# A state recurrence in three levels, meta keys' exponentials in PSUM, and pads between the experts' tiles

## The chip, the core and the metric

One core of a Trainium2 chip runs the whole kernel. The metric is device time in microseconds (us) from the first to the last instruction of one execution, as a median of runs.

## The reference, cut to what matters

```python
h = layer_norm(concat([16 meta tokens, x]))                 # (2064, 1024)
q, k, v, u, g_attn, g_ssm = split(h @ w_in)
y_attn = softmax(q k^T / 8) v                               # 8 heads, 2064 keys, the last 16 are the meta tokens
for direction in range(2):                                  # S5 layer: 32 groups x 64 complex states
    abar, bbar = zoh_discretise(a, log_dt, b)
    s_t = abar * s_{t-1} + bbar u_t                         # the state recurrence, forward and backward
    y += Re(c s)
y_ssm = gelu(y) * sigmoid(gelu(y) @ w_glu + b_glu)
h = layer_norm(alpha h + (sig(g_attn)(y_attn w1) + sig(g_ssm)(y_ssm w2)) @ w_o)
out = layer_norm(alpha h + expert_choice_moe(h))            # 16 experts, each takes its best 256 tokens
```

## The kernel before

The program is written out by hand: each engine executes its instructions in the order in which the Python code issues them, and waits only for data and for buffers.

- **Phase A** (`phase_a`) normalises 17 tiles of 128 tokens, projects them to q, k, v and u. `u_mm` (L267) makes u with matmuls of 128x128 weights against 256 columns. A float32 product is three matmuls: high part by high part, low by high, high by low.
- **Gates** (`gates`) are 64 steps of 24 matmuls of 512 columns (L1169) with nothing else to wait for than their weights' split: ACT casts the high part (L1126), DVE subtracts the low part (L1127). The generator gives control back after every 4 matmuls; such a piece is called a quantum here, and there are 384 of them. `drive` puts as many quanta behind each step of another phase as the step's `yield` says (1 if it says nothing), so the gates are TensorE's filling work in the phases `ssm` and `glu`, and in the first part of `phase_b`; what is left is issued before the main part of `phase_b`.
- **`ssm`** loads and discretises the parameters (SP's queue, L712 to L726, and DVE); makes for each chunk of 16 tokens its contribution to the state (`v_item`: 64 items, evacuated by ACT at L918 into `VA`, 129 chunks x 2 directions x 32 groups; the real half stands on partitions 0 to 63, the imaginary one on 64 to 127); runs the recurrence over the chunks (`scan`, 127 steps of 5 DVE instructions of 64 elements, one quantum behind each); and makes the outputs (`y_item`, L1009 and L1013, with the kernels of `k_item`, whose first five are combined on POOL, L879 to L881, while the scan runs). After the scan stands `yield 10`.
- **`phase_b`** sweeps 32 units (4 query blocks x 8 heads) in 9 steps each: 8 steps with 256 keys and a ninth (i = 8) with the 16 meta keys. A step makes the scores in a PSUM tile `pS` (two buffers), ACT takes the exponential into `pe` (L490) and a float16 copy `ph` (L502; in step 3 DVE makes it, L500), and `pl` = `pe` - `ph` is made by POOL (L508) for 256 keys and by DVE (L511) for the meta keys, two steps later. `max_mm` (L449) and `max_red` (L455) find the next unit's row maxima; `pend` holds at most two of them. `PROG` writes the order of a step out: S and T are the scores, M a `max_mm`, P a quarter of the products with v, and / lets DVE take the pending maxima and then one entry of its queue `vq`.
- **`experts`** takes 16 experts in turn. Weights are loaded in pieces of 1 MB, split by ACT (`wh`, L1629) and DVE (`wl`, L1630). Gate and up products (L1721) have 256 columns of `xh`/`xl` as the moving operand and 128x128 of `wh`/`wl` as weights; down products (L1749) have 256 columns of `wh`/`wl` moving and 128x128 of `hh`/`hl` as weights. All tiles in the pools `e_w` and `e_x` are whole multiples of 4 KiB per partition, and these pools follow each other directly, so any two of them start a whole number of 4 KiB apart.

Of the kernel before, what the change touches and what calls it, by code (L numbers as in the profile page):

```python
# [10 lines left out]
F32 = mybir.dt.float32  # L11
F32R = mybir.dt.float32r
# [28 lines left out]
def row_bcast(ap, n, parts=128):  # L41
    return bass.AP(tensor=ap.tensor, offset=ap.offset, ap=[[0, parts], [1, n]])
# [7 lines left out]
def kernel(ctx, tc, x, meta, ln_in_g, ln_in_b, w_in, q_norm_g, k_norm_g,  # L50
# [321 lines left out]
    def phase_b(c):  # L372
# [100 lines left out]
        def scores(n, i, a):  # L473
            g = units[n][1] // 4
            w = 2 if i < NT // 2 else 1
            m = 128 if i < NT // 2 else NM
            if a >= w:
                return
            if a == 0:
                PS[n, i] = ps.tile([128, 2, 512], F32, name="pS")  # L480
            p = PS[n, i]
            k0 = 128 * (2 * i + a)
            PE.matmul(p[:m, a], K2[g][:, k0:k0 + m], Q[n][1], start=True, stop=False)  # L483
            PE.matmul(p[:m, a], K1[g][:, k0:k0 + m], Q[n][0], start=False, stop=True)  # L484
            if a < w - 1:
                return
            e = pp.tile([128, 2, 512], F32, name="pe", bufs=PR["PE"])
            hi = pp.tile([128, 2, 512], F16, name="ph", bufs=PR["PH"])
            lo = pp.tile([128, 2, 512], F16, name="pl", bufs=PR["PH"])
            A.activation(e[:m, :w], p[:m, :w], AF.Exp, bias=ebias[:m], scale=HD ** -0.5)  # L490
            P[n, i] = e, hi, lo, m, w

        PR = dict(HI=(3,), LOV=(16,), LAG=4, LEAD=3.75, PE=7, PH=5, LOS=2,
                  PROG=("SMTM/PPP/P/M/", "SMTMPP/PP/MM/M", "SMTM//PPPP/M/M"))
# [8 lines left out]

        def split_lo(n, i, on_v):
            e, hi, lo, m, w = P[n, i]
            hs = [a for a in range(w) if (2 * i + a in PR["LOV"]) == on_v]
            if len(hs) == 2 and not on_v:
                PL.tensor_tensor(lo[:m, :w], e[:m, :w], hi[:m, :w], op=OP.subtract)  # L508
                return []
            eng = V if on_v else PL  # L510
            return [lambda a=a: eng.tensor_tensor(lo[:m, a], e[:m, a], hi[:m, a], op=OP.subtract) for a in hs]  # L511

# [79 lines left out]
        for s in range(len(steps) + LAG):  # L592
            want = min(NC, int((s + LEAD) * 20 // NP))
            live = s < len(steps)
            if live:
                n, i = steps[s]
                if i == 0 and n + 2 < NU:
                    load_q(n + 2)
            if 0 <= s - PR["LOS"] < len(steps):
                for g in split_lo(*steps[s - PR["LOS"]], False):  # L600
                    g()
                vq += split_lo(*steps[s - PR["LOS"]], True)
            if 0 < s <= len(steps) and steps[s - 1][1] in PR["HI"]:
# [31 lines left out]
            if live:  # L635
                split_hi(n, i, False)
            if s == len(steps) - 1:
                c2.close()
# [30 lines left out]
    def ssm(c):  # L669
# [6 lines left out]

        VA = tb.tile([128, 2, 32, CB + 2], F32, name="VA")
        PL.memset(VA[:, 1, :, CB:CB + 1], 0.0)
        bbar = tb.tile([128, 2, 32, 16], F32, name="bbar")
        lo_t = tb.tile([128, 2, 2, 32, T + 1], F32, name="lo_t")  # L680
        cst = tb.tile([128, 2, DG, 16], F32, name="cst")
        lt = tb.tile([128, 2, 2, 32], F32, name="lt")
        st = tb.tile([128, 2, 2, 32], F32, name="st")
        dd = tb.tile([16, 32], F32, name="dd")
# [16 lines left out]
        with pool(name="s_i", bufs=1) as ti:  # L701
# [8 lines left out]
            for i, src in enumerate((ssm_a_re, ssm_a_im)):  # L710
                for j in range(2):
                    SP.dma_start(raw[:, i, j], src.rearrange("l d g p -> (l d g) p"))  # L712
            ldt = new()
            SP.dma_start(ldt, row_bcast(ssm_log_dt, DG))
            SP.dma_start(dd, ssm_d.rearrange("l g h -> h (l g)"))
            craw = new((128, 8, 2, 2, 64), tag="gco")
            for x in range(2):
                for y in range(2):
                    src = (ssm_c_re, ssm_c_im)[x ^ y]
                    SP.dma_start(craw[:, :, x, y], src.rearrange("l d g h p -> (l d g h) p")  # L720
                                 .rearrange("(n p) q -> p n q", p=128))
# [142 lines left out]
            do(V.tensor_copy, lt, Lr[:, :, T])  # L864
            do(V.tensor_scalar, lt[64:, 1], lt[64:, 1], -1.0, None, op0=OP.mult)
            for ri in range(2):
# [5 lines left out]
            yield from flush(4)  # L872
        up = c1.enter_context(pool(name="s_u", bufs=2))
        bstv = bst.rearrange("p r (d g) h -> p r d g h", d=2)
        cstv = cst.rearrange("p r (d g) h -> p r d g h", d=2)
# [18 lines left out]
        def make_ws(i):  # L894
# [5 lines left out]
            WS[i] = ws  # L900

        def v_item(k, d, g):
            if g == 3 and d == 0 and k < 7:
                load_u(k + 1, True)
            if g == 0 and 2 * k + d < 15:
                make_ws(2 * k + d + 1)
            pw = pp.tile([128, KT, 128], F32, name="pA")
            for kt in range(KT):
                PE.transpose(pw[:, kt], WS[2 * k + d][:, g, 8 * kt:8 * kt + 8].rearrange("p j h -> p (j h)"), idf)
            yield  # L910
            wi = s1.tile([128, KT, 128], F32, name="wi", bufs=3)
            A.copy(wi, pw)
            yield
            pv = pp.tile([128, 512], F32, name="pB", bufs=3)
            for kt in range(KT):
                PE.matmul(pv[:, :CB], wi[:, kt], U[k][:, kt, g], start=(kt == 0), stop=(kt == KT - 1))
            yield
            A.copy(VA[:, d, 4 * k + g, :CB], pv[:, :CB])  # L918

        load_u(0, True)  # L920
        make_ws(0)
        yield
        for i, _ in enumerate(pipe(v_item(k, d, g) for k in range(8) for d in range(2) for g in range(4))):
            yield (i + 1) % 2
        c1.close()
        c1 = ExitStack()
        kp = c1.enter_context(pool(name="s_k", bufs=1))
        up = c1.enter_context(pool(name="s_v", bufs=2))
        CL, MM = {}, {}

# [29 lines left out]
        def load_mm(k):  # L960
            mm = kp.tile([128, KT, 2, TH], F32, name="mm", bufs=3)
            for g in range(2):
                for kt in range(KT):
                    src = kf_d[2 * k + g]
                    SP.dma_start(mm[:, kt, g], bass.AP(tensor=src.tensor, offset=src.offset + 8 * kt * 16,
                                                       ap=[[16, 8], [NL * 16, 16], [1, TH]]))
            MM[k] = mm

        def slot(f, bk, p0, p1):
            a = VA[p0:p1, :, :, f]  # L970
            ap = [list(z) for z in a.ap]
            ap[1][0] += bk - f
            return bass.AP(tensor=a.tensor, offset=a.offset, ap=ap)

        def scan():
            for m in range(1, CB - 1):
                f0, f1 = m - 1, m
                b0, b1 = CB - m, CB - 1 - m
                tt(st[:, 0], lt[:, 0], slot(f0, b0, 0, 128), OP.mult)
                tt(st[:64, 1], lt[64:, 1], slot(f0, b0, 64, 128), OP.mult)  # L980
                tt(st[64:, 1], lt[:64, 1], slot(f0, b0, 0, 64), OP.mult)
                cur = slot(f1, b1, 0, 128)
                tt(cur, cur, st[:, 0], OP.add)
                tt(cur, cur, st[:, 1], OP.add)
                yield

        kk = pipe((k_item(k, False) for k in range(5)), every=22)
        for _ in scan():
            next(kk, None)
            yield  # L990
        for _ in kk:
# [6 lines left out]
        def y_item(k):  # L998
            if k % 2 == 0 and k < 14:
                load_u(k // 2 + 1, False)  # L1000
            py = pp.tile([128, 2, KT, CX], F32, name="pB", bufs=3)
            mm, cl = MM.pop(k), CL.pop(k)
            u = U[k // 2]
            for g in range(2):
                ug = 2 * (k % 2) + g
                for mt in range(KT):
# [3 lines left out]
                    for d in range(2):  # L1010
                        w = cl[:, d, g, 1 - d:T + 1 - d].rearrange("p j h -> p (j h)")
                        a0 = 2 * d
                        PE.matmul(py[:, g, mt], w[:, cs_], VA[:, d, 2 * k + g, a0:a0 + CX], start=False, stop=d == 1)  # L1013
                yield
            t = kp.tile([128, 2, KT, CX], F32, name="yt", bufs=3)
            A.activation(t, py, AF.Square)
            yield
            V.tensor_scalar(t, t, 0.044715, 1.0, op0=OP.mult, op1=OP.add)
# [590 lines left out]

    def experts(c, pos, inf):  # L1610
        wp = c.enter_context(pool(name="e_w", bufs=3))
        E0 = E - 7
# [35 lines left out]
        yield first_split()  # L1648
        xp = c.enter_context(pool(name="e_x", bufs=2))
        sm = c.enter_context(pool(name="e_m", bufs=2))  # L1650
        pp = c.enter_context(pool(name="e_p", bufs=2, space=PSUM))
# [50 lines left out]
        def trans_out(e, i, p):  # L1702
            if i == 0:
                XT[e] = (xp.tile([128, 8, CAP], F32R, name="xh"), xp.tile([128, 8, CAP], F32R, name="xl"))
            hi, lo = XT[e]
# [351 lines left out]
```

## Time and profile before

| | us |
|---|---|
| median of 3 runs | 3305.42 |
| lowest, highest run | 3301.82, 3309.93 |
| the profiled execution | 3306.01 |
| its span (first to last instruction) | 3303.9 |

The span is what the trace covers; the profiled execution is 2.1 us longer than its span and 0.6 us longer than the median. Engines in the rows: PE is TensorE's matmuls, PEld its weight loads, DVE VectorE, ACT ScalarE, POOL GpSimd, SP SyncE, and a q behind a name the engine's queue of issues and waits. L12 is line 12 of the kernel before.

### The profile page before, as it was taken

The page shows a single profiled execution, that of the slowest core. Times are in us where ns is not written, and L with a number is a line of the kernel's source. Part 1 is how long each engine was busy: PE and PEld are TensorE (multiplying, and loading weights), DVE is VectorE, ACT ScalarE, POOL GpSimd, SP SyncE. Part 2 cuts the span into 40 slices and gives each one's busy share as a digit, 9 for nine tenths or more (in the row PEclk, how much of TensorE's full clock was granted, in tenths as well). Part 3 has the DMA queues.
Part 4 walks back from the last instruction along what each step waited for, and adds up shares of the span by engine and source line. Part 5 has one row for each costly group of instructions (what it writes and reads, how often), then busy time and mean ns, then how long its engine had stood idle before and what let it go on. Part 6 is the DMA issues. An engine that isn't in the chain of part 4 may idle for free. (4 is left out here: it accounts for less than half of the span.)

```text
span 3303.9 us, 56603 instructions
## 1 busy us (share of the span) xinstructions
PE 3045.8 (92%) x22805; PEld 2686.9 (81%) x22805; DVE 2287.5 (69%) x4206; ACT 1557.3 (47%) x2197; POOL 1000.7 (30%) x633
## 2 busy tenths in 40 slices
PE   6999996788999999999999997599999999999997
PEld 5887785566777777777778886599999999999997
DVE  7884779985357777777556665666566665778875
ACT  2222341112349889898732222344444444556552
POOL 3221050033039989898820001000011001112221
PEclk9999998899999999999999998799999999999998
DMA  6666521544730101012086652366666666878773
GB/s 223 192 193 213 132 77 53 163 131 139 217 109 21 33 21 33 17 36 86 27 254 191 175 169 104 110 210 203 204 205 214 208 204 217 262 235 281 262 255 133
DMA packets 464502, 513.03 MB, mean 155 GB/s; under 512 B 47568, under 2 KB 387728, under 8 KB 463856
## 3 DMA queue, kind: packets, MB, share of 16 engines
q1 hardware_dynamic: 435104, 422.31, 40.4%
q0 software_dynamic: 19232, 69.53, 7.2%
q10 hardware_dynamic: 9904, 17.57, 1.5%
q8 instruction: 179, 2.93, 0.4%
q14 instruction: 83, 0.68, 0.1%
HBM read 385.59 MB, written 123.76 MB: 154 GB/s over the span
## 5 line engine op out<-in xcount | busy, mean ns | idle before, releaser
L1721 PE MATMUL pg<-xh,wh 128*128 128x256 f32 x2048 | 586.3, 286 | 15.7 <-DVE sg L1729 9.7
L1721 PE MATMUL pg<-xh,wl 128*128 128x256 f32 x2048 | 582.8, 285 | 0.5 <-DVE wl L1630 0.5
L1721 PE MATMUL pg<-xl,wh 128*128 128x256 f32 x2048 | 582.9, 285 | 0.0
L1630 DVE TENSOR_TENSOR wl<-wr,wh 128x2048 fp32r<-128x2048 f32 x189 | 433.1, 2292 | 215.1 <-ACT wh L1629 215.1
L508 POOL TENSOR_TENSOR pl<-pe,ph 128x1024 f16<-128x1024 f32 x256 | 554.6, 2201 | 79.7 <-DVE ph L500 67.1
L455 DVE TENSOR_REDUCE mx<-pm 128x1 f32<-128x412 f32 (+1 forms) x640 | 365.5, 584 | 153.6 <-PE pm L449 138.3
L1721 PEld LDWEIGHTS pg<-xh,wh 128*128 128x128 f32 x2048 | 396.6, 194 | 17.0 <-issue 12.2
L1721 PEld LDWEIGHTS pg<-xh,wl 128*128 128x128 f32 x2048 | 396.6, 194 | 0.7 <-DVE wl L1630 0.7
L1721 PEld LDWEIGHTS pg<-xl,wh 128*128 128x128 f32 x2048 | 396.8, 194 | 0.0
L1629 ACT CAST wh<-wr 128x2048 fp32r<-128x2048 f32 x189 | 358.4, 1896 | 7.3 <-DMA wr<-in_w_up_e_dram 5.7
L1169 PE MATMUL pg<-gh,gwh 128*128 128x512 f32 x1024 | 344.8, 412 | 12.9 <-ACT gg L1140 6.9
L490 ACT ACTIVATE pe<-pS,ebias 128x1024 f32<-128x1024 f32 (+1 forms) x288 | 306.6, 1065 | 63.3 <-PE pS L484 62.6
L1749 PE MATMUL pd<-wh,hh 128*128 128x256 f32 x1024 | 292.6, 286 | 5.2 <-ACT ye L1767 2.7
L1749 PE MATMUL pd<-wh,hl 128*128 128x256 f32 x1024 | 290.5, 284 | 0.7 <-DVE hl L1736 0.7
L1749 PE MATMUL pd<-wl,hh 128*128 128x256 f32 x1024 | 290.2, 283 | 0.0
L1169 PE MATMUL pg<-gh,gwl 128*128 128x512 f32 x512 | 213.0, 416 | 63.0 <-DVE gwl L1127 62.9
L449 PE MATMUL pm<-k,q 128*128 128x412 f32 (+1 forms) x640 | 237.7, 381 | 33.4 <-DVE mx L455 29.0
L502 ACT CAST ph<-pe 128x1024 f16<-128x1024 f32 (+1 forms) x256 | 254.2, 993 | 18.3
L1169 PEld LDWEIGHTS pg<-gh,gwh 128*128 128x128 f32 x1024 | 200.1, 198 | 59.8 <-ACT gg L1140 8.8
L525 PEld LDWEIGHTS <-ph 128*128 128x128 f16 (+1 forms) x2176 | 190.5, 97 | 65.0 <-issue 61.8
L525 PE MATMUL po<-v,ph 128*128 128x129 f16 (+1 forms) x2176 | 234.0, 222 | 0.7 <-ACT t L533 0.7
L483 PE MATMUL pS<-q,k 128*128 128x512 f32 (+1 forms) x544 | 232.7, 428 | 0.0
(412 smaller groups left out, 6848.7 us busy)
## 6 DMA issues: line engine op xcount, KB each, us to landing
wr<-in_w_gate_e_dram SPq DMA_DIRECT2D x64, 1024.0 KB
wr<-in_w_up_e_dram SPq DMA_DIRECT2D x64, 1024.0 KB
wr<-in_w_down_e_dram SPq DMA_DIRECT2D x64, 1024.0 KB
gwr<-in_w_in_dram SPq DMA_DIRECT2D x32, 512.0 KB
gh<-ht_d SPq DMA_DIRECT2D x64, 256.0 KB
gt_d<-gg ACTq DMA_DIRECT2D x64, 256.0 KB
gt<-gt_d SPq DMA_DIRECT2D x32, 512.0 KB
q<-q_d SPq DMA_DIRECT2D x96, 128.0 KB
```

The costliest lines, as they stand in the source:

```text
L449: PE.matmul(p[:, :w], Q[n][0][:, 128 * j:128 * j + 128], K1[units[n][1] // 4][:, k0:k0 + w], start=True, stop=True)
L455: V.tensor_reduce(MX[n][:, j, c:c + 1], p[:, :w], axis=AX.X, op=OP.max)
L483: PE.matmul(p[:m, a], K2[g][:, k0:k0 + m], Q[n][1], start=True, stop=False)
L490: A.activation(e[:m, :w], p[:m, :w], AF.Exp, bias=ebias[:m], scale=HD ** -0.5)
L502: A.copy(hi[:m, :w], e[:m, :w])
L508: PL.tensor_tensor(lo[:m, :w], e[:m, :w], hi[:m, :w], op=OP.subtract)
L525: PE.matmul(o[:, 0:129], hi[:m, a, 128 * j:128 * j + 128], v16[:m, kt, g, 0:129], start=(kt == 0 and j % 2 == 0), stop=False, skip_group_c ...
L1169: PE.matmul(p, w[:, k], h, start=(k == 0 and j == 0), stop=(k == 7 and j == 2))
L1629: A.copy(wh, wr)
L1630: V.tensor_tensor(wl, wr, f(wh), op=OP.subtract)
L1721: PE.matmul(p[:, gu], w[:, k, cs_], x[:, k], start=(k == 0 and j == 0), stop=(k == 7 and j == 2))
L1749: PE.matmul(p, a[:, k, cs_], w[:, k], start=(k == 0 and j == 0), stop=(k == 7 and j == 2))
```

## The change

1. **Scan.** `VA` is laid out chunk first (chunk, direction, group), the backward direction written and read in reverse. The 128 chunks are 16 segments of 8. Level 1 does the 7 inner steps of all segments together (7 x 5 DVE instructions of 16x64 elements); level 2 carries the segments' ends (15 x 5 of 64); level 3 adds the carries to the inner chunks (5 x 5 of 3x7x64). The coefficients are the powers 1 to 8 of the step's factor (`powers`, DVE, issued in pieces between the items that fill `VA`). Behind each instruction of levels 1 and 3 stand 2 quanta of gates, behind each step of level 2 one. The first five `k_item`s start every 12 yields instead of 22.
2. **Outputs.** `y_item` reads a copy of its two groups' states (`take_vs`, two ACT copies of 256 elements for each k, two k ahead). The tiles `mm` and `yt` and the `u` buffers now come from pools opened after the scan's own, so their loads come after it.
3. **Parameters.** Nine loads (a, log dt, c) go through ACT's queue instead of SP's.
4. **Meta keys.** Their exponential is written into the unused half of the scores' PSUM tile, and DVE's subtraction stands at the front of its queue one step earlier; the tile is free only after it.
5. **Experts.** A tile of 32 bytes stands ahead of `e_w`; `xh` and `xl` move to a pool of their own, behind a tile of 64 bytes that follows `e_x`.

```diff
-            e = pp.tile([128, 2, 512], F32, name="pe", bufs=PR["PE"])
+            e = pp.tile([128, 2, 512], F32, name="pe", bufs=PR["PE"]) if w == 2 else p[:, 1:]
...
+        def split_lo(n, i):
+            (PL if w == 2 else V).tensor_tensor(lo[:m, :w], e[:m, :w], hi[:m, :w], op=OP.subtract)
...
+            if 0 <= s - PR["LOS"] < len(steps) and steps[s - PR["LOS"]][1] < NP - 1:
+                split_lo(*steps[s - PR["LOS"]])
...
                 split_hi(n, i, False)
+                if i == NP - 1:
+                    vq.insert(0, lambda st=steps[s]: split_lo(*st))
...
-        VA = tb.tile([128, 2, 32, CB + 2], F32, name="VA")
+        VA = tb.tile([128, CB + 1, 2, 32], F32, name="VA")
...
-                    SP.dma_start(raw[:, i, j], src.rearrange("l d g p -> (l d g) p"))
+                    A.dma_start(raw[:, i, j], src.rearrange("l d g p -> (l d g) p"))
...
+        def powers():
+            V.tensor_copy(pw[:, :, 0], lt.rearrange("p r d g -> p r (d g)"))
+            n = 1
+            while n < SL:
+                a, b = [pw[:, r, n - 1:n].to_broadcast([128, n, 64]) for r in range(2)]
+                for x0, x1, o, op in ((0, 1, 0, OP.subtract), (1, 0, 1, OP.add)):
+                    V.tensor_tensor(pt[:, 0, :n], pw[:, x0, 0:n], a, op=OP.mult)
+                    V.tensor_tensor(pt[:, 1, :n], pw[:, x1, 0:n], b, op=OP.mult)
+                    V.tensor_tensor(pw[:, o, n:2 * n], pt[:, 0, :n], pt[:, 1, :n], op=op)
+                    yield
+                n *= 2
...
-            A.copy(VA[:, d, 4 * k + g, :CB], pv[:, :CB])
+            dst = VA[:, 1:, d, 4 * k + g]
+            A.copy(back(dst, CB) if d else dst, pv[:, :CB])
...
+        def take_vs(k):
+            VS[k] = yp.tile([128, 2, 2, CX], F32, name="vs", bufs=2)
+            for d in range(2):
+                src = VA[:, 1 - d:1 - d + CX, d, 2 * k:2 * k + 2]
+                A.copy(VS[k][:, d].rearrange("p g c -> p c g"), back(src, CX) if d else src)
...
-                tt(st[:, 0], lt[:, 0], slot(f0, b0, 0, 128), OP.mult)
-                tt(st[:64, 1], lt[64:, 1], slot(f0, b0, 64, 128), OP.mult)
-                tt(st[64:, 1], lt[:64, 1], slot(f0, b0, 0, 64), OP.mult)
-                cur = slot(f1, b1, 0, 128)
-                tt(cur, cur, st[:, 0], OP.add)
-                tt(cur, cur, st[:, 1], OP.add)
...
+            def step(coef, prev, cur, dims):      # the same five instructions, on dims elements
...
+            for j in range(1, SL):
+                dims = [NS, 64]
+                coef = [wide(z[:, r, 0:1], dims) for r in range(2)]
+                for _ in step(coef, v[:, j - 1], v[:, j], dims):
+                    yield 2
+            for s in range(1, NS):
+                for _ in step([z[:, r, SL - 1] for r in range(2)], v[:, SL - 1, s - 1], v[:, SL - 1, s], [64]):
+                    pass
+                yield
+            B = 3
+            for s in range(1, NS, B):
+                dims = [B, SL - 1, 64]
+                coef = [wide(z[:, r, None, 0:SL - 1], dims) for r in range(2)]
+                prev = wide(v[:, SL - 1, s - 1:s - 1 + B, None], dims)
+                cur = v[:, 0:SL - 1, s:s + B].rearrange("p j s x -> p s j x")
+                for _ in step(coef, prev, cur, dims):
+                    yield 2
...
+        c.enter_context(pool(name="e_pad", bufs=1)).tile([128, 8], F32, name="skew")
         wp = c.enter_context(pool(name="e_w", bufs=3))
...
         xp = c.enter_context(pool(name="e_x", bufs=2))
+        c.enter_context(pool(name="e_skew", bufs=1)).tile([128, 16], F32, name="skew")
+        tp = c.enter_context(pool(name="e_xt", bufs=2))
...
-                XT[e] = (xp.tile([128, 8, CAP], F32R, name="xh"), xp.tile([128, 8, CAP], F32R, name="xl"))
+                XT[e] = (tp.tile([128, 8, CAP], F32R, name="xh"), tp.tile([128, 8, CAP], F32R, name="xl"))
```

## Rows read from the trace of the kernel before

**Rows 1.** The page: busy time, share and instructions of each engine.
```profile
PE 3045.8 (92%) x22805; PEld 2686.9 (81%) x22805; DVE 2287.5 (69%) x4206; ACT 1557.3 (47%) x2197; POOL 1000.7 (30%) x633
```

**Rows 2.** Stretches: length, busy PE, PEld, DVE, ACT, POOL, clock, DMA, GB/s.
```profile
400.00:471.60 71.60, 71.60 (x506) 65.89 (x505) 53.75 (x47) 43.60 (x134) 24.14 (x29) 1.00 0.32 97
471.60:500.00 28.40, 24.30 (x100) 18.54 (x99) 27.81 (x24) 5.30 (x8) 27.77 (x24) 0.94 0.10 36
...
471.60:693.30 221.70, 157.51 (x591) 118.84 (x590) 204.13 (x650) 30.61 (x45) 28.91 (x24) 0.84 0.33 104
```

**Rows 3.** The scan's stretch, the gates' matmuls (L1169) alone: PE, PEld, clock, DMA.
```profile
471.60:693.30 221.70, 148.42 (x551) 115.12 (x549) 0.84 0.33 104
```

**Rows 4.** Who waited for whom from 471.6 to 693: us, times, longest.
```profile
PE pg L1169 <- DVE gwl L1127: 62.4, 10, 13.9
```

**Rows 5.** DVE in order of time: wide products, the scan beside POOL, the scan alone.
```profile
408.74 1.22 DVE L879 TENSOR_TENSOR ws<-go_t,bst 128x1024 f32<-128x1024 f32 x1
409.87 1.26 DVE L879 TENSOR_TENSOR wt<-go_t,bst 128x1024 f32<-128x1024 f32 x1
...
483.32 3.58 DVE L675 TENSOR_TENSOR st<-lt,VA 128x64 f32<-128x64 f32 x3
...
600.05 0.85 DVE L675 TENSOR_TENSOR st<-lt,VA 128x64 f32<-128x64 f32 x3
...
601.54 0.84 DVE L675 TENSOR_TENSOR st<-lt,VA 128x64 f32<-128x64 f32 x3
```

**Rows 6.** PE in order of time: gates' matmuls without a wait.
```profile
545.33 0.62 PE L1169 MATMUL pg<-gh,gwh 128*128 128x512 f32 x2
...
546.01 0.62 PE L1169 MATMUL pg<-gh,gwh 128*128 128x512 f32 x2
```

**Rows 7.** SP's queue, then PE, in order of time, where the parameters load.
```profile
338.05 6.87 SPq L724 DMA_DIRECT2D bst<-in_ssm_b_im_dram  x2
...
350.93 31.01 SPq L1119 DMA_DIRECT2D gwr<-in_w_in_dram  x5
...
356.48 0.73 PE L1169 MATMUL pg<-gh,gwh 128*128 128x512 f32 x2 [3.41 <-ACT gg L1140]
```

**Rows 8.** PE in order of time: the gates' last matmul.
```profile
965.83 0.39 PE L1169 MATMUL pg<-gh,gwl 128*128 128x512 f32 x1
```

**Rows 9.** DVE lines, ns min/median/max: meta keys; q and k from PSUM; from SBUF.
```profile
L511 DVE TENSOR_TENSOR pl<-pe,ph x32: 670/2692/8021, 990.0 to 1636.7; 16x512 f16<-16x512 f32 x32
...
L232 DVE TENSOR_TENSOR sq<-pq,gs x32: 479/481/484, 57.6 to 290.7; 128x320 f32<-128x320 f32 x32
...
L234 DVE TENSOR_TENSOR qn<-qn,rs x16: 825/2062/2076, 60.0 to 292.1; 128x640 f32<-128x640 f32 x16
```

**Rows 10.** Who waited for whom from 968 to 1640: us, times, longest.
```profile
PE pm L449 <- DVE mx L455: 28.7, 28, 5.8
```

**Rows 11.** One unit's end and the next one's start, in order of time.
```profile
1023.98 3.07 DVE L455 TENSOR_REDUCE mx<-pm 128x1 f32<-128x412 f32 x5 [1.18 <-PE pm L449]
...
1025.29 0.62 ACT L502 CAST ph<-pe 16x512 f16<-16x512 f32 x1
...
1026.97 0.48 PE L483 MATMUL pS<-q,k 128*128 128x512 f32 x1
...
1029.05 2.69 DVE L511 TENSOR_TENSOR pl<-pe,ph 16x512 f16<-16x512 f32 x1
```

**Rows 12.** Experts' stage, gate and up matmuls alone: stretch, PE, PEld, clock, DMA.
```profile
2100.00:3304.00 1204.00, 756.07 (x6144) 747.94 (x6144) 0.98 0.68 219
...
2500.00:2505.00 5.00, 5.00 (x44) 5.00 (x43) 1.00 0.52 180
```

**Rows 13.** Phase A, u's matmuls (L267) alone, in two bursts: columns as above.
```profile
85.60:90.60 5.00, 5.00 (x45) 5.00 (x44) 1.00 0.12 34
101.70:106.70 5.00, 5.00 (x47) 5.00 (x46) 1.00 1.02 328
```

**Rows 14.** Experts, PE in order of time: two gate and up matmuls ten apart.
```profile
2113.13 0.28 PE L1721 MATMUL pg<-xl,wh 128*128 128x256 f32 x1
...
2114.33 0.28 PE L1721 MATMUL pg<-xh,wl 128*128 128x256 f32 x1
```

## The prediction on record

> **What bounds the kernel now.** I read the page's list of engines first: TensorE is busy for 92% of the span [rows 1], so an edit is worth what it takes out of PE's own work or out of PE's waits, and nothing else. Then I read the table of stretches, looking for places where PE loses time. The stage before the scan (400 to 471.6) has PE busy without a gap at clock 1.00 [rows 2]; the scan (471.6 to 693.3, 221.7 us) has not: 157.5 us busy at a mean clock of 0.84. Of that, 148.4 us are 551 matmuls of the gates [rows 3] and 9.1 us the kernels of `k_item`. At full clock a gates' matmul takes 0.227 us (three starts in 0.68 us) and a quantum of four 0.907 us [rows 6], so the 551 would need 125 us, and PE loses about 221.7 - 125 - 9 = 88 us here. The table of waits names the cause: ten waits of PE for `gwl`, 62.4 us together [rows 4]. That is DVE's subtraction at L1127, which stands in DVE's queue behind scan steps. A step of five small instructions takes 1.49 us (one start to the next) [rows 5] and carries one quantum; a gates' step of six quanta thus takes 6 x 1.49 = 8.9 us on DVE and 5.4 us on PE. So DVE paces this stretch: 127 x 1.49 = 189 us, some 22 us in which 24 instructions of POOL hold DVE up (24 DVE instructions fill the 28.4 us to 500, 1.17 us each, against 0.28 alone [rows 2, 5]), and 11 splits of about 1.1 us, the spacing of DVE's products of 1024 elements [rows 5].
>
> In phase b the table of waits shows PE waiting 28.7 us for `mx` [rows 10], DVE's reduction; DVE is late there because of L511. In the experts PE has no gap, but 44 matmuls of 256 columns start in 5 us [rows 12]: 120 ns each (the last one's length of 0.28 added: 5.28/44), and ten starts in 1.20 us say the same [rows 14].
>
> **The scan.** Level 1 has 35 instructions of 16x64 = 1024 elements. The row for that size is 1.13 us [rows 5]: 41 us with the start of a dependent one. POOL's 24 instructions of the same stretch hold DVE up as before, about 1.1 us each: +26. Six splits: +7. DVE 74 us. PE has 70 quanta x 0.907 = 63.5, plus 3.6 of `k_item`: 67. Level 2 has 15 steps x 1.49 = 22.5, plus one split: 24 us on DVE, 15 on PE. Level 3 has 25 instructions of 3x7x64 = 1344 elements, 1.48 us each by that size: 37, and four splits 4.6: 42 on DVE; on PE 50 quanta x 0.907 + 3.6 = 49. The generators couple both queues within a dozen quanta, since a gates' step needs its split; I let the slower one set each level: 74 + 24 + 49 = 147, plus the ten quanta behind it (9) and a microsecond of start: 157 instead of 221.7, so -65. Bounds: queues that run past each other freely, 150 (-72); PE at half clock through level 2 and part of level 3, because level 2 leaves it only 15 of 24 us, 181 (-41). The row for that fall is the 0.84 [rows 2].
>
> What this moves: the scan takes 135 quanta instead of 127, so the gates run out eight earlier. They end at 965.8 now, just before phase b's main part [rows 8], where what is left is issued anyway; DVE's first reductions (0.61 us each [rows 11]) then bound that stretch. The eight are worth 7.3 us at most and nothing at least; I take -3.
>
> **Outputs, powers, parameters.** The loads of `u` and `mm` start only after the scan, behind ten quanta (9 us) that hide most of it: +3 (0 to +8). The copies of `take_vs` go to ACT, idle then. The gates' reloads of weights have less time in a faster scan: +3. The powers are 20 small instructions in a stretch where DVE is busy 53.8 of 71.6 us and PE all of it [rows 2]; PE hides them unless an item waits: +1 (0 to +7). VA's strided copies fall on ACT, 43.6 of 71.6 us busy: nothing. SP's queue issues the parameters ahead of the gates' next `gwr` (one issue of two takes 6.87 us, the next five of `gwr` 31 us), and PE idles 3.4 us in that stretch [rows 7]; with nine loads on ACT's queue SP comes to `gwr` earlier: -2 (0 to -3.4). Behind ACT's nine issues stand the gates' casts (L1126), which PE waits for, and that keeps it from the full 3.4.
>
> **Meta keys.** L511 takes 0.67 to 8.0 us, 2.69 in the median [rows 9]. At 1029.05 it takes 2.69 with nothing to do but 512 columns [rows 11]. The q and k products that read PSUM (L232) stay within 479 to 484 ns, while those that read SBUF only (L234) spread from 825 to 2076 [rows 9]. So I take L511 at its minimum of 0.67 once its source is in PSUM, and all 28.7 us of waits for `mx` are gone. But the tile `pS` is now held until the subtraction is done. At the unit's boundary five reductions stand ahead of it, which end at 1023.98 + 3.07 = 1027.05; with 0.67 behind them the tile comes free at 1027.7. PE writes the next unit's scores at 1026.97 [rows 11]: 0.8 us late, in 32 units +25. Net -3. Bounds: no new wait, -29; an operation that still takes 2.69, so 2.8 us late in each unit, 90 - 29 = +61.
>
> **Experts' pads.** Before, moving tile and weights start a whole number of 4 KiB apart, and gate and up products take 120 ns. The nearest row of the same shape (128x128 weights, 256 columns, full clock) is L267 in phase A: 45 and 47 matmuls in 5 us, (5 + 0.28)/45 = 117.3 and 112.3 ns [rows 13]. By the declarations its moving tile and weights start 64 bytes off each other modulo 128, and so will `xh` against `wh` after the change; `hh` against `wh` (the down products) stays at a whole multiple. So 6144 of the 9216 matmuls may fall by 2.7 to 7.7 ns; I take 4 (the slower burst is the steadier row): -25. Bounds 0 and 6144 x 7 = -43.
>
> A rule speaks against this term. The Trainium skill ("TensorE: Matmul & The Clock Gate", section "Step-by-step: what each phase is for") says that the moving operand and the weight load come through two independent SBUF read ports, and that loading the next weights takes no read bandwidth from the running matmul; by it, where tiles start would not matter and the term would be 0. This trace bears it out only in part: the same shape runs at 120 ns here and at 112 to 117 there [rows 12, 13].
>
> **Sum.** -65 - 3 + 3 + 3 + 1 - 2 - 3 - 25 = -91, against the profiled execution's 3306.0: 3215, and 3214 against the median, which is 0.6 lower.
>
> **Rivals.** *The pads do nothing*: the 5 ns between L267 and L1721 come from something else, such as transfers (DMA busy 0.52 of the experts' burst, but 1.02 in the fastest L267 burst, which speaks against it [rows 12, 13]). 3306 - 66 = 3240. The rule of the Trainium skill named above ("TensorE: Matmul & The Clock Gate") is this rival. *The scan keeps half the throttle*: clock at 0.84 or below in levels 2 and 3, only 41 saved: 3239. For it speaks that gaps and low clock went together before; against it that level 1, by the sum, leaves PE nearly full. *The subtraction still queues behind POOL*: PSUM source or not, it also reads `ph` and writes `pl` in SBUF, and holds `pS` for 2.7 us in each unit: +61 in place of -3, 3279. *Slower*: the new offset lengthens the experts' interval. At 256 columns and 2.4 GHz the columns alone take 106.7 ns; 13.3 of the 120 are overhead. All else gives -66, so it decides from 66/9216 = 7.2 ns more on every expert matmul; with that overhead doubled the kernel takes 3240 + 123 = 3363. For it: start addresses would matter, as the faster rows suggest. Against: L267 at that offset is faster.
>
> **Chances and range.** Forecast 0.55 (its own range 3190 to 3235); pads nothing 0.22; scan 0.08; meta held 0.07; slower 0.04; several losses that cancel, no change, 0.04. A difference of 0.3%, about 10 us, is what a measurement of this kernel can tell from none; by that bound faster 0.92, same 0.04, slower 0.04. The range reaches up past the second and third cases with their own spread of 25, and down by 7 (scan at -72), 18 (pads at -43) and 11 (the meta keys half-way to their best): 3178 to 3265.
>
> **What would show it.** The scan: its stretch near 157 us, clock near 1.00 except in level 2, hardly a wait for `gwl`. Level 1's instructions near 1.13 us without POOL. Meta keys: the subtraction at 0.67 us, no long waits for `mx`, instead about 32 waits of S for the subtraction near 0.8 us. Pads: 5 us of gate and up matmuls hold 45 or 46 instead of 44, down products unchanged. Wrong would make it above all that strided or broadcast operands in level 1 and 3 cost more than 1.13 us for 1024 elements (at 2 us level 1 alone would be 30 us longer), or that `pS` is held longer than 0.8 us.

## The result and the profile after

The changed kernel takes 3193.94 us (median of 4, 3192.74 to 3195.53) against 3305.73 for the kernel before (median of 4, the profiled execution with it): ratio 0.9662, 95% interval 0.9645 to 0.9679, or 112 us off. The prediction said 3214 (91 off), range 3178 to 3265.

Cut at instructions that both traces have, by their start in each (span 3303.9 and 3191.1):

| stretch of TensorE's work | before | after | difference | prediction |
|---|---|---|---|---|
| start to the last product that fills `VA` | 471.0 | 478.8 | +7.8 | -1 |
| from there (the scan) to the first output product | 222.3 | 148.2 | -74.1 | -65 |
| outputs, glu, start of phase b, to its first scores | 272.8 | 272.1 | -0.7 | +3 |
| phase b to the first product of the merge | 673.3 | 645.9 | -27.4 | -3 |
| merge and choice of tokens, to the first expert product | 469.9 | 470.9 | +1.0 | 0 |
| experts to the end | 1194.6 | 1175.2 | -19.4 | -25 |

The scan, with its three levels, in the table of stretches (length, then PE, PEld, DVE, ACT, POOL, clock, DMA share, GB/s), beside [rows 2]:

```profile
480.00:552.00 72.00, 71.29 (x312) 55.23 (x311) 70.99 (x46) 16.23 (x24) 47.86 (x24) 1.00 0.35 112
552.00:572.00 20.00, 19.55 (x82) 14.04 (x80) 17.97 (x80) 3.66 (x6) 0.00 (x0) 1.00 0.96 290
572.00:614.00 42.00, 40.50 (x172) 31.27 (x173) 39.87 (x31) 8.90 (x13) 0.00 (x0) 1.00 0.50 154
...
478.80:626.80 148.00, 145.33 (x626) 112.17 (x625) 134.17 (x157) 33.49 (x52) 49.06 (x25) 1.00 0.49 151
```

PE is busy for 96 to 99% of every level, and the granted clock is 1.00 throughout; before, the mean was 0.84. Who waited for whom there, against the 62.4 us of [rows 4]:

```profile
PE pg L1230 <- DMA gh<-ht_d: 1.9, 5, 0.7
PE pg L1230 <- DVE gwl L1188: 0.7, 1, 0.7
```

DVE in order of time: level 1 beside POOL, level 1 after POOL has finished, level 2, level 3.

```profile
487.61 2.03 DVE L1015 TENSOR_TENSOR VA<-VA,st 128x1024 f32<-128x1024 f32 x1
...
543.30 1.23 DVE L1017 TENSOR_TENSOR VA<-VA,st 128x1024 f32<-128x1024 f32 x1
...
559.57 0.22 DVE L1009 TENSOR_TENSOR st<-pw,VA 128x64 f32<-128x64 f32 x1
...
573.80 1.55 DVE L1011 TENSOR_TENSOR st<-pw,VA 64x1344 f32<-64x1344 f32 x1
```

The meta keys: DVE's subtraction (ns min/median/max), against 670/2692/8021 in [rows 9], and PE's two largest waits of phase b beside [rows 10]:

```profile
L506 DVE TENSOR_TENSOR pl<-pS,ph x32: 668/668/679, 922.9 to 1538.7; 16x512 f16<-16x512 f32 x32
```
```profile
PE pS L483 <- ACT pe L490: 9.1, 30, 0.3
PE pm L449 <- DVE mx L455: 2.1, 3, 1.5
```

The experts' gate and up products, to be read beside 756.07 us for the same 6144 in [rows 12], then the down products alone, before and after:

```profile
2006.00:3191.00 1185.00, 732.86 (x6144) 724.66 (x6144) 0.98 0.70 223
```
```profile
2100.00:3304.00 1204.00, 376.28 (x3072) 371.55 (x3072) 0.98 0.68 219
```
```profile
2006.00:3191.00 1185.00, 374.98 (x3072) 370.14 (x3072) 0.98 0.70 223
```

And the one stretch that lost: ACT issues the nine parameter loads from 316.87 to 328.77, and PE waits 12.47 us for the sigmoid behind them. Its load of a table (1.28 us) is no part of the loss: the kernel before has it too, with the sigmoid at 318.59. ACT's queue, then PE:

```profile
316.87 3.08 ACTq L708 DMA_DIRECT2D s<-in_ssm_a_re_dram  x2
320.17 1.84 ACTq L708 DMA_DIRECT2D s<-in_ssm_a_im_dram  x2
...
328.40 0.37 ACTq L716 DMA_DIRECT2D s<-in_ssm_c_re_dram  x1
328.80 1.28 ACT L1201 ACT_TABLE_LOAD   x1 [12.72 <-DMA s<-in_ssm_c_re_dram]
330.10 0.60 ACT L1201 ACTIVATE gg<-pg 128x512 f32<-128x512 f32 x1
```
```profile
330.75 1.22 PE L1230 MATMUL pg<-gh,gwh 128*128 128x512 f32 x2 [12.47 <-ACT gg L1201]
```

### The profile page after: what moved, and what is told of

It is laid out like the page before. It is cut to its first block, busy times and chain, and to the rows that moved or that the text cites. A ratio compares the mean times of both kernels' runs of the same rounds, so it can differ in the third digit from the quotient of the medians.

```text
span 3191.1 us, 56127 instructions
## 1 busy us (share of the span) xinstructions
PE 2993.2 (94%) x22805; PEld 2649.9 (83%) x22805; DVE 2149.0 (67%) x3725; ACT 1569.8 (49%) x2229; POOL 1006.6 (32%) x633
## 5 line engine op out<-in xcount | busy, mean ns | idle before, releaser
L1785 PE MATMUL pg<-xh,wh 128*128 128x256 f32 x2048 | 576.2, 281 | 18.2 <-DVE sg L1793 11.7
L1785 PE MATMUL pg<-xh,wl 128*128 128x256 f32 x2048 | 572.6, 280 | 1.1 <-DVE wl L1692 1.1
L1785 PE MATMUL pg<-xl,wh 128*128 128x256 f32 x2048 | 572.9, 280 | 0.0
L506 POOL TENSOR_TENSOR pl<-pe,ph 128x1024 f16<-128x1024 f32 x256 | 542.3, 2148 | 61.5 <-DVE ph L500 49.3
L1785 PEld LDWEIGHTS pg<-xh,wl 128*128 128x128 f32 x2048 | 386.9, 189 | 1.3 <-DVE wl L1692 1.3
L1785 PEld LDWEIGHTS pg<-xl,wh 128*128 128x128 f32 x2048 | 387.6, 189 | 0.0
L1230 PE MATMUL pg<-gh,gwh 128*128 128x512 f32 x1024 | 331.3, 399 | 23.4 <-ACT gg L1201 19.8
L490 ACT ACTIVATE pe<-pS,ebias 128x1024 f32<-128x1024 f32 x256 | 284.5, 1111 | 39.6 <-PE pS L484 39.6
L502 ACT CAST ph<-pe 128x1024 f16<-128x1024 f32 x224 | 234.4, 1046 | 15.6
L522 PE MATMUL po<-v,pl 128*128 128x65 f16 (+1 forms) x2176 | 221.8, 193 | 2.2 <-POOL pl L506 2.1
```

The source lines that it names most:

```text
L502: A.copy(hi[:m, :w], e[:m, :w])
L506: (PL if w == 2 else V).tensor_tensor(lo[:m, :w], e[:m, :w], hi[:m, :w], op=OP.subtract)
L1230: PE.matmul(p, w[:, k], h, start=(k == 0 and j == 0), stop=(k == 7 and j == 2))
L1785: PE.matmul(p[:, gu], w[:, k, cs_], x[:, k], start=(k == 0 and j == 0), stop=(k == 7 and j == 2))
```

## The experiments

The kernel before was timed again beside each group of experiments, and its median lay between 3305.73 and 3312.97 us; kernels are therefore compared by their ratios to it.

**Each part alone, on the kernel before.** Four kernels: before plus the scan part (with powers and output copies), plus the meta keys' part, plus the pads, plus the parameter loads; each with the lines of the diff that are its own and no others.

> The kernel before with the three-level scan alone (powers and output copies included; parameters on SP's queue, meta keys and experts as before). Theory A: once DVE no longer holds up the gates, TensorE's own work paces everything up to phase b, and that stretch is PE-bound: 148 us between the last item that fills VA and the first output product instead of 222, and 72 to 76 us off the whole. Theory B (the prediction's sum): each level is paced by the slower of DVE and PE, 157 us and about 65 off the whole.

> The kernel before with the meta keys' exponential in PSUM and DVE's subtraction at the front of its queue, nothing else. Theory A: PE's waits for the row maxima go (28.7 us to about 2), and the held tile is wanted only one step later, so nothing new of that size replaces them: 25 to 29 us off. Theory B (the prediction's sum): 0.8 us of new wait in each unit gives 25 of the 29 back: about 3 off.

> The kernel before with the experts' pads alone. Theory A: gate and up products start every 117.5 ns instead of 120, down products stay, 15 to 20 us off. Theory B: where tiles start does not matter, and the shorter interval in the changed kernel comes from something else in it: 0.

> The kernel before with nine parameter loads on ACT's queue, nothing else. Theory A: ACT issues them ahead of the gates' sigmoid, PE waits about 12 us for that once, and the kernel is 6 to 10 us slower. Theory B (the prediction's sum): SP comes earlier to the gates' weights, 2 to 3 us faster.

| part alone | ratio to before, 95% interval | us off, medians |
|---|---|---|
| scan | 0.9771 (0.9754 to 0.9788) | 75.2 |
| meta keys | 0.9904 (0.9887 to 0.9921) | 32.6 |
| pads | 0.9939 (0.9921 to 0.9957) | 22.0 |
| parameters | 1.0023 (1.0014 to 1.0033) | -6.9 |

The product of the ratios is 0.964, against 0.9662 of the whole change: within the intervals the parts add up. The scan gives theory A's 72 to 76 (its interval, 70 to 81 us, leaves out the prediction's 65), with a stretch of 150.8 us instead of A's 148. The meta keys give some 33, ten times the prediction's sum. The pads' 22.0 us are a little more than theory A's 15 to 20. The parameters make the kernel slower, through PE's wait for `gg`, 14.7 us at its longest (16.6 in all, 4.3 before):

```profile
PE pg L1169 <- ACT gg L1140: 16.6, 4, 14.7
```

**What paces the scan.** This kernel leaves out POOL's 30 products beside level 1; a fill with zeros takes their place:

```diff
...
-                combine(eng, cl[:, d], ct, lo_t, cstv, d, 2 * k, 2, T + 1)
+                if fast:
+                    combine(eng, cl[:, d], ct, lo_t, cstv, d, 2 * k, 2, T + 1)
+                else:
+                    PL.memset(cl[:, d], 0.0)
```

> The changed kernel with part of the work left out: POOL's 30 products that combine the first five kernels beside level 1 are replaced by a fill with zeros, so those kernels are wrong. Level 1's instructions should fall from 2.03 to 1.23 us each, some 20 to 26 us less work for DVE. Theory A (the stretch is bound by PE, DVE has that much slack): the stretch of the scan stays within 3 us of 148 and the kernel within 5 us of the changed one. Theory B (each level is paced by the slower engine, as the prediction summed it): level 1 falls from 73 to PE's 67 or less and the kernel is 7 to 20 us faster than the changed one.

Ratio 0.9652 (0.9635 to 0.9668), not to be told from 0.9662. The stretch, from its last product that fills `VA` to the first output product:

```profile
480.90:627.80 146.90, 144.84 (x627) 112.51 (x626) 113.33 (x157) 33.52 (x52) 2.60 (x6) 1.00 0.49 153
```

DVE has 21 us less to do (113.3 instead of 134.2), and the stretch is 1.3 us shorter, with PE busy for 144.8 us as it was (145.3): PE sets it, theory A.

**Source or place of the subtraction.** In the changed kernel, the exponential back in SBUF:

```diff
-            e = pp.tile([128, 2, 512], F32, name="pe", bufs=PR["PE"]) if w == 2 else p[:, 1:]
+            e = pp.tile([128, 2, 512], F32, name="pe", bufs=PR["PE"])
```

> The changed kernel with one thing undone: the meta keys' exponential goes to a tile in SBUF again, while DVE's subtraction stays one step earlier at the front of its queue. Theory A (the source counts: from SBUF the operation is held up by POOL's work): the subtraction takes 0.7 to 8 us again, 2.7 in the median, PE's waits for the row maxima come back to 15 us or more, the kernel is 12 to 30 us slower than the changed one (ratio 0.970 to 0.975 of before). Theory B (the place in the queue counts): waits stay near 2 us, no difference (ratio 0.966).

```profile
L506 DVE TENSOR_TENSOR pl<-pe,ph x32: 1434/2668/7987, 921.1 to 1562.4; 16x512 f16<-16x512 f32 x32
```
```profile
PE pm L449 <- DVE mx L455: 30.5, 34, 5.8
```

Ratio 0.9755 (0.9739 to 0.9771), about 31 us more than with PSUM: the source counts. The earlier place by itself takes nothing off the waits for `mx` (30.5 us, 28.7 before). The waits of S for ACT are gone here too, so they belong to the held tile.

**The pads.** Three kernels: without the 32 bytes ahead of the weights; with other offsets; and with 64 bytes for the down products too, together with the parameters on SP's queue (a's loads are shown; those of log dt and c go likewise):

```diff
-        c.enter_context(pool(name="e_pad", bufs=1)).tile([128, 8], F32, name="skew")
```
```diff
-        c.enter_context(pool(name="e_skew", bufs=1)).tile([128, 16], F32, name="skew")
+        c.enter_context(pool(name="e_skew", bufs=1)).tile([128, 8], F32, name="skew")
...
+        c.enter_context(pool(name="e_skew2", bufs=1)).tile([128, 16], F32, name="skew")
+        hp = c.enter_context(pool(name="e_ht", bufs=1))
...
-                HT[e] = (xp.tile([128, 8, CAP], F32R, name="hh", bufs=1), xp.tile([128, 8, CAP], F32R, name="hl", bufs=1))
+                HT[e] = (hp.tile([128, 8, CAP], F32R, name="hh", bufs=1), hp.tile([128, 8, CAP], F32R, name="hl", bufs=1))
```
```diff
-                    A.dma_start(raw[:, i, j], src.rearrange("l d g p -> (l d g) p"))
+                    SP.dma_start(raw[:, i, j], src.rearrange("l d g p -> (l d g) p"))
...
-                HT[e] = (xp.tile([128, 8, CAP], F32R, name="hh", bufs=1), xp.tile([128, 8, CAP], F32R, name="hl", bufs=1))
+                HT[e] = (tp.tile([128, 8, CAP], F32R, name="hh", bufs=1), tp.tile([128, 8, CAP], F32R, name="hl", bufs=1))
```

> The changed kernel without the 32 bytes ahead of the weights' pool; the 64 bytes ahead of xh and xl stay, so that the offset between moving tile and weights is the same. Theory A (only the offset counts): gate and up products stay at 116 to 117.5 ns and the stage within 2 us. Theory B (the absolute position counts too): the interval goes up by 1 ns or more, 6 us or more in the stage.

> The changed kernel with other offsets between moving tiles and weights, modulo 128 bytes: 32 for gate and up products, 96 for down products (64 and 0 in the changed kernel). Theory A (any offset that is not a whole 128 bytes helps alike): both at 116 to 117.5 ns, down products 3 ns shorter. Theory B (the offset of 64 is special): gate and up products go back towards 120 ns or beyond, some 15 us more in that stage.

> The changed kernel with two edits: parameters on SP's queue again, and hh and hl moved into the pool of xh and xl, so that the down products too have 64 bytes between moving tile and weights. Theory A: PE's wait of 12.5 us for the gates' sigmoid goes (6 to 9 us), and down products start every 116 to 117.5 ns instead of 120 (3072 of them: 8 to 12 us), together 14 to 21 us faster than the changed kernel, ratio about 0.961. Theory B (the wait is replaced by one for the gates' weights, and the offset of the down products does not matter because the tiles in the other role are moving): within 5 us of the changed kernel.

PE's busy time in the table of stretches, restricted to one line, over the whole stage (6144 gate and up products, 3072 down products):

| offset gate and up / down, bytes mod 128 | gate and up, us | down, us |
|---|---|---|
| 0 / 0 (before) | 756.07 | 376.28 |
| 64 / 0 (changed kernel) | 732.86 | 374.98 |
| 64 / 0, pads alone | 733.71 | 376.41 |
| 64 / 0, no first pad | 736.12 | 376.49 |
| 32 / 96 | 736.15 | 367.97 |
| 64 / 64 (parameters on SP) | 731.38 | 362.67 |

The rows of the last two kernels, gate and up, then down, with 32 and 96 bytes, and down with 64:

```profile
2000.00:3320.00 1320.00, 736.15 (x6144) 728.10 (x6144) 0.98 0.63 201
```
```profile
2000.00:3320.00 1320.00, 367.97 (x3072) 362.92 (x3072) 0.98 0.63 201
```
```profile
2000.00:3320.00 1320.00, 362.67 (x3072) 357.15 (x3072) 0.98 0.62 199
```

The kernels without the first pad and with 32 and 96 bytes ran once each (3192.72 and 3188.78 us) and count here by their traces alone. The effect follows the offset wherever it is applied: 3.2 to 4.0 ns for each gate and up product at 64 bytes, and (376.28 - 362.67)/3072 = 4.4 ns for each down product, whose tiles play the other roles. 32 bytes give 3.2 ns, which is not to be told from 64 without the first pad; 96 give the down products 2.7 ns, most of the 4.4. From start to start, in the median of the traces, gate and up products are 120 ns apart at offset 0 and 117 at 64 and at 32, down products 120 at 0, 115 at 64 and 117 at 96. So theory A (any offset helps) holds, "alike" only roughly. Without the first pad the gate and up products take 3.3 us more, between the 2 of that run's theory A and the 6 of its theory B; kernels with that pad differ by 2.3 at one offset, so it may be worth nothing. The last kernel of the table takes 3173.51 us, ratio 0.9602 (0.9586 to 0.9618); its last product for `VA` starts at 469.9, 8.9 us before the changed kernel's.

**Two more steps on that kernel that brought nothing**: the parameters on POOL's queue, and a pad of 64 bytes between the gates' tiles.

```diff
-                    SP.dma_start(raw[:, i, j], src.rearrange("l d g p -> (l d g) p"))
+                    PL.dma_start(raw[:, i, j], src.rearrange("l d g p -> (l d g) p"))
```
```diff
+        c.enter_context(pool(name="g_skew", bufs=1, side="right")).tile([128, 16], F32, name="skew")
         wp = c.enter_context(pool(name="g_w", bufs=2, side="right"))
```

> As params_back_and_down_pad (the changed kernel, 64 bytes of offset for the down products too), but with the nine parameter loads on POOL's queue, which has no work there. Theory A (loads on a queue with nothing behind them free SP earlier for the gates' weights): the last item that fills VA comes 2 to 5 us earlier than with SP's queue (469.9), the kernel 2 to 5 us faster than that one, ratio about 0.959. Theory B (the loads themselves are late on that queue, and DVE's discretisation waits for them): it comes later than 469.9, 0 to 8 us slower.

> As params_back_and_down_pad, with 64 bytes of offset between the gates' moving tiles and their weights as well (matmuls of 512 columns, 227 ns at offset 0). Theory A (the offset saves a fixed 3 to 4 ns per matmul whatever its columns): the interval falls to 223 or 224 ns, 1536 of them give 4 to 6 us. Theory B (at 512 columns the weight load is hidden and the offset does not matter, or 227 is the best there is): 226 ns or more, no gain, 0 to 6 us slower.

On POOL's queue the last product for `VA` starts at 475.0, 5.1 us later than with SP's, as theory B has it, but not for theory B's reason: the loads are issued by 328.9, earlier than on SP's queue (335.3). DVE is late all the same: its discretisation starts at 345.5 instead of 337.5, behind a split `gwl` that waits 22.5 us instead of 16.1 for ACT's `gwh`, and ends 5.1 us later. PE's waits for `gh` grow from 2.7 to 7.3 us there. The ratio, 0.9598 (0.9578 to 0.9618), does not tell it from 0.9602. The gates' 1536 matmuls of 512 columns take 384.23 us with the pad and 384.20 without, from start to start 230 and 227 ns in the median (ratio 0.9591, 0.9573 to 0.9609): no gain, theory B. With the pad, then without:

```profile
301.00:899.00 598.00, 384.23 (x1536) 281.43 (x1536) 0.99 0.52 156
```
```profile
301.00:899.00 598.00, 384.20 (x1536) 284.43 (x1536) 0.98 0.53 155
```

**Why the held tile costs little.** On the same kernel, the subtraction issued ahead of the next unit's first exponential:

```diff
+                    if s and s <= len(steps) and steps[s - 1][1] == NP - 1:
+                        split_lo(*steps[s - 1])
                     if live:
                         scores(n, i, 1)
...
-                if i == NP - 1:
-                    vq.insert(0, lambda st=steps[s]: split_lo(*st))
```

> As params_back_and_down_pad, with DVE's subtraction for the meta keys issued before the next unit's first exponential instead of after it, so that the tile it holds comes round in turn: the second scores of a unit go into that tile, and wait for the subtraction, instead of into the tile of the first scores, where they wait for that exponential (30 waits of 0.3 us, 9.1 us in all, in the changed kernel). Theory A (the waits come from the order in which the two buffers come free): the 0.3 us waits for ACT go, waits for the subtraction stay under 4 us in all, 5 to 9 us faster than params_back_and_down_pad (ratio about 0.958). Theory B (the tile is then wanted as soon as the prediction said): PE waits 0.3 to 0.8 us for the subtraction in each unit, and the kernel is the same or up to 20 us slower.

3160.24 us, ratio 0.9563 (0.9547 to 0.9579): some 13 us, more than the 5 to 9 of theory A, and the fastest of all. S no longer waits for ACT; for the subtraction there is one wait:

```profile
PE pS L483 <- DVE pl L506: 0.8, 1, 0.8
```

## Why the prediction came out as it did

The median is 20 us below the forecast (22 by the table of stretches). The terms were further off than that and partly cancel, which is luck: the scan gave 9 us more than forecast, phase b 24 and the outputs with the start of phase b 4, while the first stretch lost 9, the experts gave 6 less and the merge lost 1.

**The scan** was sized mostly from DVE, and its DVE terms held within 4 us: level 1 from 479.6 to 552 (72.4 us, 74 in the sum), level 2 20 us (24), level 3 to 617.7 (45.5 us with its splits; the sum had 42 on DVE and 49 on PE). The step that failed is "I let the slower one set each level". The queues ran past each other freely, PE had no wait of more than 0.7 us for `gwl`, and the stretch came out as PE's own work, 145.3 busy of 148. That it fell close to the prediction's lower bound of 150 is partly luck: that bound is the sum of DVE's terms (74 + 24 + 42, and 10 behind them), while PE's terms make only 67 + 15 + 49 + 9 = 140. PE needed 5 us more than that, mostly since the gates' products took 0.234 us each (136.5/583) instead of 0.227; why was not traced. POOL's 26 us in level 1 were real on DVE, 21 as measured (2.03 instead of 1.23 us an instruction), and worth no more than 1.3 us in the stretch, as the kernel with POOL idle shows.

**The meta keys** were the largest miss. The half that rested on rows was right: 668 to 679 ns at all 32 instances, and 2.1 us of waits for `mx` left of 28.7. The Trainium skill ("SBUF — State Buffer", section "🔬 SBUF: two separate sides") says that a DVE operation with two inputs in SBUF and a GpSimd operation that reads SBUF take a shared port pair in turns; 668 ns from PSUM against 2668 from SBUF, in the same place of the queue, agrees. The failed step is "PE writes the next unit's scores at 1026.97 [rows 11]: 0.8 us late": it assumed that those scores go to the held tile. The changed kernel's boundary, DVE, ACT and PE in order of time:

```profile
939.81 3.06 DVE L455 TENSOR_REDUCE mx<-pm 128x1 f32<-128x412 f32 x5 [1.12 <-PE pm L449]
942.79 0.67 DVE L506 TENSOR_TENSOR pl<-pS,ph 16x512 f16<-16x512 f32 x1
```
```profile
942.09 1.11 ACT L490 ACTIVATE pe<-pS,ebias 128x1024 f32<-128x1024 f32 x1 [0.43 <-PE pS L484]
```
```profile
943.26 0.50 PE L483 MATMUL pS<-q,k 128*128 128x512 f32 x1 [0.30 <-ACT pe L490]
...
945.38 0.48 PE L483 MATMUL pS<-q,k 128*128 128x512 f32 x1
```

The reductions end at 942.87 and the subtraction at 943.46, as the prediction had it. But the scores at 943.26 start before that: they wait for the exponential of the step before (942.09 + 1.11 = 943.20), so they go into that step's tile, whose last use stands first in program order, and the held one is used at 945.38, 1.9 us after it is free. The price of holding is thus 30 waits of 0.30 us, 9.1 in all, in place of 25. Of phase b's 27.4 us, 20.1 are idle time of PE (38.1 to 18.0) and 7.3 busy time for the same products, at a mean clock of 0.99 instead of 0.98; the prediction counted waits alone.

With the subtraction issued earlier the waits for ACT are gone, and phase b, from its first to its last step's scores, takes 621.2 us instead of 634.6. Of these 13.4 us, 8.8 are idle time of PE (15.4 to 6.6); the other 4.6, busy time for the same products, were not traced to a cause. The held tile does come round in turn here: at the first boundary the new unit's second scores start at 913.91, after the subtraction's end at 913.49 and before the end of the exponential of the step before (913.21 + 1.12 = 914.33). But the kernel changes a second thing: on DVE the subtraction stands behind three reductions instead of five:

```profile
930.31 1.76 DVE L455 TENSOR_REDUCE mx<-pm 128x1 f32<-128x412 f32 x3 [1.12 <-PE pm L449]
932.19 0.68 DVE L506 TENSOR_TENSOR pl<-pS,ph 16x512 f16<-16x512 f32 x1
```

Behind five, the held tile in turn would have kept PE from 942.96 (943.26 less its wait) to 943.46, 0.5 us in this unit, so the prediction's 0.8 was not far off for a tile that was not the one handed out.

**The parameters** had the sign wrong. The prediction named what stands behind ACT's issues ("the gates' casts (L1126), which PE waits for") and took 1.4 us off for it (-2 instead of -3.4); it is the sigmoid L1201 rather than the cast that stands there, and it starts at 330.1 instead of 318.6. SP, whose relief was counted as a gain, was not what PE waited for: [rows 7] puts its 3.41 us down to ACT's `gg`. Loads back on SP's queue undo it.

**The experts** were a little over-sized: -23.2 us in the gate and up products (25 predicted), -1.3 in the down products, and about 5 of these lost again, as PE was idle that much longer in the stage. The products of 256 columns fall by about 4 ns at an offset of 64 bytes; at 512 columns no gain from the offset was seen. The Trainium skill ("TensorE: Matmul & The Clock Gate", section "Step-by-step: what each phase is for") says that PE has two independent read ports and that weight loads take no read bandwidth from the running matmul. The rival that the prediction drew from it, that the pads would do nothing, is refuted at 256 columns; whether the rule itself fails is not shown, since why the offset acts was not tried.

**Small terms.** Outputs, reloads and the eight quanta came to -0.7 instead of +3. The quanta run out at 891.6, 7.5 us before the first scores, and PE is idle for 6.6 us in the last 39.4 us there (0.9 in 38.4 before): most of the 7.3 us of matmuls that moved from there into the scan came back as idle time. The powers cost nothing: from first to last, the products for `VA` take 72.5 us (72.4 before).

## What to carry to other kernels

When filling work couples two queues, count the stretch by the total of each engine first; a sum of the slower engine by stage holds only if neither can run ahead. A buffer held longer is paid for at the next request that really gets it: find out which tile the pool hands out, and issue the last use of a held one in the order in which it should come round. Before loads are moved to an idle queue, look at the first instruction behind them, however little that engine has to do.

## What the runs showed of the hardware that was not expected

A DVE operation with one input in PSUM ran 32 times within 668 to 679 ns beside a POOL that was busy for 574 of 636 us; with both inputs in SBUF the same took 1434 to 7987. The time of float32r products of 256 columns depends on where moving tile and weights start relative to each other: 123.1 ns of PE's busy time each at 0 (756.07/6144), 119.3 at 64 in the changed kernel (732.86/6144), and 119.8 at 32 (736.15/6144), within what kernels at 64 differ by; the same 64 bytes gained nothing for 512 columns.
